# Where two gates get their sigmoid, and which of seven products waits for the last input: a hybrid attention and recurrence layer

## The chip, the cores and the metric

The kernel runs on one core of a Trainium2 chip. The metric is the time of one execution in microseconds (us); every time below is of the device. A core has engines that run at the same time and meet through semaphores: PE (TensorE, matrix products; PEld is its weight load), ACT (ScalarE, activation functions and copies), DVE (VectorE, elementwise), POOL (GpSimd, elementwise and some DMAs) and SP, which only issues DMAs. Each engine works through its own queue strictly in order. ACT computes a function from a table that has to be loaded first; a load shows in the profile as ACT_TABLE_LOAD.

## The reference, cut to what matters

One layer over 1024 tokens of width 1024. One input projection feeds everything; the parts that the change touches are the two SiLU gates `silu(g) = g * sigmoid(g)` and the last projection.

```python
h = rms_norm(h_res, norm_w[layer])
z = einsum('bsd,dc->bsc', h, w_in)                       # one projection, cut into pieces
qkv_a, g_a, q_b, zf_fwd, zf_bwd, i_b, g_b, zgate_a, zgate_b = split(z, split_points)
# (A) three groups of dilated window attention, q and k RMS-normed, merged by their denominators
y_a = einsum('bsc,cd->bsd', o_a * silu(g_a), w_proj_a)
# (B) gated linear recurrence with heads of 128, forward and backward, in chunks
f = lb + (1.0 - lb) * sigmoid(z_f); log_f = log(f)       # its decay, used through exp
o_b = rms_norm(o_fwd + o_bwd, hg_norm_w) * silu(g_b)
y_b = einsum('bsc,cd->bsd', o_b, w_proj_b)
merged = sigmoid(zgate_a) * y_a + sigmoid(zgate_b) * y_b
h_res = h_res + einsum('bsd,de->bse', merged, w_out)
```

## The kernel before

**Precision and pages.** Every wide product is made in three: both operands are split into a high part (a copy by ACT into a reduced format: `whi`, `xh`) and a low part (the difference, by POOL, DVE or ACT with a DMA: `wlo`, `xl`), and PE multiplies high by high, high by low and low by high. Weights come in pages of 128 by 512; nine split pages stand ready (`RING`).

**The order is planned at build time.** The class `Plan` (L115) keeps a model clock for each engine, and `Builder` emits instructions by it: work that hangs on other engines is a task with a priority, given out by `tick` (L263) when the model says that its inputs are about ready. Small products of PE are put between the large ones by `burst` (L279) under the same rule, with a slack of 0.6 us. On the chip the emitted order is fixed; only semaphores delay it. The model gives a change of ACT's table 1.28 us (`note`, L141), and counts `exp` as served by the set that also has `ln`.

**Stages**, by the time in the profile:

1. 0 to 150 us: normalisation of the input, values of attention.
2. The block stage, 149.6 to 730.2 us (`run_quads`, L444). 24 blocks of the projection, each made by Strassen's scheme in Winograd's form: seven products instead of eight (`11`, `T1`, `T2`, `21`, `T3`, `22`, `T4`), in PSUM banks named qA, qE and qC. Three products share one bank, so `T2` may only start when ACT has copied `11` out of it. Weight sums on DVE (`qraw`) go ahead of the split. Twelve blocks are queries and keys (`put_qk`): each quarter of the block goes through a square, a head sum on PE (`nss`), an inverse root by `Ln` and `Exp` on ACT (`guess`, L1090; both write `ny`) and a Newton step on DVE (L1097). Six blocks are merge gates, stored raw (`put_sg`, L1116). Four blocks are the SiLU gate of the recurrence (`gb`) and two that of attention (`ga`), the last two of the stage: for these `put_ga` (L1129) sends each of the 24 quarters through a sigmoid on ACT and a product on DVE (`ga_sig`, L1143), and then to DRAM (`gaD`, `gbD`).
3. Attention, 747 to 945 us, with large products of the next stage's inputs between its small ones (`gp` groups on PE).
4. The merge of the three groups, up to 1034 us (`merge_load`, L1474): eight pieces, each with three loads and the gate from `gaD`, into `oaD`.
5. The recurrence, 1040 to about 1355 us. Eight heads, each about 36 us. On ACT a head is: four sigmoids over `sk` and, after a preload of the set that has `ln` and `exp`, four `Ln` (both in `logs`, L1676), sixteen `Exp` for keys and queries (`exps_b`, L1705: `km`, `qr`, `q`), and in the output norm twice a `Ln` and an `Exp` of 128 by 4 (`oy`). PE turns keys (`kT`), makes states (`U`), cross terms (`X`, `Y`) and outputs (`oB`), and `out_transpose` (L1913) takes the output (`onT`) times the gate loaded into one of two `gb` buffers (L1612). Other rings: eight `qr`, four `km`. Between them PE runs `gp` groups of 24 products.
6. 1355 to 1583 us: the rest of the merge gates, the attention projection, then the projection of the recurrence and the output projection, each by seven products in the order `SEVEN` (L1999; `seven_weights`, `seven_sides` and `seven`, L2018 to L2097). The first writes `sA` and `sE`; its quarters times their gates, added to the other branch's, are the tiles `ma`, inputs of the second. `seven_sides(M)`, which splits these, is called after all of the first projection has been emitted (L2233).

Of the kernel before, what the change touches and what calls it, by code (L numbers as in the profile page):

```python
# [583 lines left out]
def hybrid_block(ctx, tc, a, out):  # L584
# [530 lines left out]

    def put_sg(w, j):  # L1116
        def f(half, col, z, mine):
            ring = stage
            if not mine:
                ring, ps, z = blk["spare"], z, blk["spare"].get()  # L1120
                a_.activation(z, ps, AF.Copy)

            def out():
                s_.dma_start(sgD[w, j + col, half], z)
                ring.done(z)
            b.task("sp", [z], out, 1)
        return f

    def put_ga(j, dst=None):  # L1129
        dst = gaD if dst is None else dst  # L1130

        def f(half, col, z, mine):
            ring = stage
            if not mine:
                ring, ps, z = blk["spare"], z, blk["spare"].get()
                a_.activation(z, ps, AF.Copy)
            b.task("act", [z], lambda: ga_sig(dst[j + col, half], z, ring), 3, blk["y"].soon)
        return f

    def put_gb(pr):  # L1140
        return put_ga(2 * pr, gbD)

    def ga_sig(dst, z, ring):  # L1143
        t = blk["y"].get()
        a_.activation(t, z, AF.Sigmoid)

        def mul():
            v_.tensor_tensor(z, z, t, op=OP.mult)
            blk["y"].done(t)
            b.task("sp", [z], out, 1)  # L1150

        def out():
            s_.dma_start(dst, z)
            ring.done(z)
        b.task("dve", [t], mul, 3)

# [238 lines left out]
    def merge_maybe(now=False):  # L1395
        if mer or not (now or len(stored) == 48) or not att:
            return
        if now:
            b.drain()
        b.eager, b.SLACK = False, 0.6  # L1400
        psum(3)
        actx.close()
        mer["p"] = mctx.enter_context(tc.tile_pool(name="merge", bufs=1))
        mer["sel"] = sel = mer["p"].tile([16, 4, 128], F32R, name="sel")
        half = lambda k: ident[0:16, 8 * k:8 * k + 8].rearrange("p (a j) -> p a j", a=4)[:, :, :, None].to_broadcast([16, 4, 2, 64])
        v_.tensor_tensor(sel.rearrange("p a (j c) -> p a j c", j=2), half(0), half(1), op=OP.add)
        mer["og"] = b.ring(mer["p"], "og", 6, [128, 512])
        mer["gal"] = b.ring(mer["p"], "gal", 2, [128, 512])
        merge_start()

# [213 lines left out]
    IG = {}  # L1624
    GB = {}
    H = {}
# [42 lines left out]
    def start_head(h):  # L1669
# [35 lines left out]
    def exps_b(h, d, u, D1, Q2):  # L1705
# [199 lines left out]
    def scale_out(h, u, ps, on, r):  # L1905
        for c in range(4):
# [91 lines left out]

    SEVEN = ("11", "21", "T2", "T1", "T3", "22", "T4")  # L1999

    def near(tiles):
# [4 lines left out]

    def in_order(work):

# [6 lines left out]
        for k, (op, eng, ready, f) in enumerate(work):  # L2015
            b.task(eng, [], lambda f=f: go(f), 2 + 0.1 * SEVEN.index(op), lambda k=k, ready=ready: at[0] == k and ready())

    def seven_weights(base, pages, along=None):  # L2018
        raw = {}
# [4 lines left out]

        for op in SEVEN:
            for i in range(4):
# [15 lines left out]

        for op in SEVEN:
            for i in range(4):
                split(op, i)
        in_order(work)

    def seven_sides(X):
        pairs, work, mixes, did, s2, spent = {}, [], [], set(), {}, set()

        def free2(i):
            if i in spent:
                acc.done(s2[i])
# [13 lines left out]
        def mix(op, i, dst, x, y, how, after=()):  # L2067
            def f():
                if op == "T2":
                    s2[i] = acc.get()  # L2070
                if op == "T2":
                    v_.scalar_tensor_tensor(s2[i], X[*x, i], -1.0, X[*y, i], op0=OP.mult, op1=OP.subtract)
# [3 lines left out]
                if op == "22":  # L2076
# [3 lines left out]
            mixes.append((op, "dve", lambda: all((*k, i) in X for k in at) and all((m, i) in pairs for m in after)  # L2080
                          and near([X[*k, i] for k in at]) and (op != "T2" or acc.soon()), f))

        for op, a, kh in (("11", 0, 0), ("21", 0, 1), ("T2", 0, 0), ("T1", 1, 0), ("T3", 0, 0), ("22", 0, 1), ("T4", 1, 1)):
            for i in range(4):
                split(op, kh, a, i)
# [3 lines left out]
        for i in range(4):  # L2089
            mix("22", i, (0, 1), (0, 1), "s2", OP.add, ("21",))  # L2090
        for i in range(4):
            mix("T1", i, (1, 0), (1, 0), (1, 1), OP.subtract)
        in_order(work)
        in_order(mixes)
        return pairs

    def seven(base, pairs, tok, A, E, kept, fin, ready):  # L2097

# [32 lines left out]

        for o, op in enumerate(SEVEN):
            for u in range(4):
# [56 lines left out]
    b.low = "dve"  # L2190
    seven_weights(b.ops, quad[0], {"11": obs})
    pairs_b = seven_sides(X)

# [14 lines left out]
    pos += 8  # L2208
    seven_weights(b.ops + 28, quad[1])

    def fin_b(half, c, u, t, bank_):
# [24 lines left out]

    def x_load(u):
        t = sgr.get()
        s_.dma_start(t, a["x"][4 + u, :, 0:512])
        xr[u] = t  # L2240
# [4 lines left out]
    def fold(op, u, t):  # L2245
        half, e = {"11": (0, 0), "T1": (1, 1)}.get(op, (0, 1))

        def f():
            more(t, a["x"][4 * half + u, :, 512 * e:512 * e + 512])
            folded.add((op, u))  # L2250
# [5 lines left out]
    def fin_o(half, e, u, t, bank_):  # L2256
        r0 = 128 * (4 * half + u)
        ring, o = acc, t
# [10 lines left out]
        def late():  # L2269
            more(o, a["x"][u, :, 512:1024])  # L2270
            b.task("sp", [o], out_, 1)
# [4 lines left out]

    seven(b.ops + 28, pairs_o, True, b.bank, b.gps, fold, fin_o, lambda op, u: (op, u) in folded)
    b.drain()
# [103 lines left out]
```

## Time and profile before

| | us |
|---|---|
| three runs | 1585.03, 1586.14, 1587.09 (median 1586.14) |
| the profiled execution | 1584.98, of which the span from first to last instruction 1583.2 |
| PE busy in the span | 1489.0 (94%) |
| ACT busy | 994.3 (63%), in it 107 table loads: 137.3 |
| DVE busy | 975.7 (62%) |
| POOL busy | 365.6 (23%) |

Busy is the time in which an engine had at least one instruction running; a row of the groups gives an instruction's tiles (written before the arrow, read after it), its shape, its count, busy time, the mean of one in ns, and the idle time of the engine just ahead of it with what ended that. A row of the windows gives start and end, length, then the busy time and count of each engine, the mean granted PE clock (1.00 is full), the DMA share and GB/s. A wait reads "who <- what ended it: total us, times, longest".

### The profile page before, as it was taken

To read this page: it belongs to the slowest core of one execution; us is meant where nothing else is said; L and a number is where in the kernel's file an instruction comes from. 1 tells how busy PE (TensorE), PEld (TensorE's weight loads), DVE (VectorE), ACT (ScalarE), POOL (GpSimd) and SP (SyncE) were. 2 spreads that over 40 slices of the span, in tenths; PEclk is the share of its full clock that TensorE was granted. 3 is DMA by queue.
4 is the path that set the end of the run, shared out by engine and by line. 5 is a ranking of instruction groups with operands and counts; after the bars stand their busy time and mean duration, and the time that the engine had idled before them with its cause. 6 is when DMAs were issued, how large, how long until landed. Compare 5 with 4: busy or idle time off the path is not lost.

```text
span 1583.2 us, 23063 instructions
## 1 busy us (share of the span) xinstructions
PE 1489.0 (94%) x7965; PEld 1216.0 (77%) x7965; DVE 975.7 (62%) x1890; ACT 994.3 (63%) x1963; POOL 365.6 (23%) x376
## 2 busy tenths in 40 slices
PE   8999999798798889689999999999999999998998
PEld 7788887576676667567888878788888888876787
DVE  6792676466556767563554332628888877358873
ACT  5543667667767788774676762157877875546451
POOL 0032344244232322122030032332222222000011
PEclk9999999899999999899999999999999999999999
DMA  5365466455313323127654446863446443664554
GB/s 192 131 197 194 162 200 135 140 133 113 107 67 107 100 57 103 47 80 235 217 195 160 134 133 165 249 178 87 121 100 166 108 120 101 207 223 148 166 143 131
DMA packets 193578, 227.76 MB, mean 144 GB/s; under 512 B 45563, under 2 KB 118291, under 8 KB 192948
## 3 DMA queue, kind: packets, MB, share of 16 engines
q1 hardware_dynamic: 174084, 204.06, 39.6%
q0 software_dynamic: 11952, 21.76, 8.8%
q10 hardware_dynamic: 7424, 0.45, 0.3%
q8 instruction: 63, 1.03, 0.3%
q14 instruction: 55, 0.45, 0.1%
HBM read 166.08 MB, written 81.63 MB: 156 GB/s over the span
## 4 chain that ended last, share of the span: by engine, by line
PE 58%; ACT 9%; issue 4%; DVE 4%; DMA 1%; SPq 0%; POOL 0%; ACTq 0%; DVEq 0%; POOLq 0%
PE gp L57 26%; PE qA L57 7%; PE sA L57 5%; PE sE L57 3%; ACT L57 3%; PE o L57 3%; ACT ny L57 3%; PE oB L57 2%; PE qE L57 2%; PE sc L57 2%; PE pT L57 2%; ACT whi L57 1%; PE U L57 1%; PE qC L57 1%; PE X L57 1%
## 5 line engine op out<-in xcount | busy, mean ns | idle before, releaser
L57 POOL TENSOR_TENSOR wlo<-qraw,whi 128x512 fp32r<-128x512 f32 x120 | 170.5, 1427 | 403.2 <-ACT whi L57 376.8
L57 ACT ACTIVATE whi<-qraw 128x512 fp32r<-128x512 f32 x168 | 103.1, 624 | 66.0 <-DVE qraw L57 36.2
L57 ACT ACT_TABLE_LOAD x107 | 137.3, 1283 | 8.6 <-PE gp L57 5.5
L57 PE MATMUL gp<-hh,whi 128*128 128x512 f32 x336 | 138.3, 412 | 0.7 <-ACT stage L57 0.7
L57 PE MATMUL gp<-hh,wlo 128*128 128x512 f32 x336 | 131.6, 392 | 0.0
L57 PE MATMUL gp<-hl,whi 128*128 128x512 f32 x336 | 131.1, 390 | 0.0
L57 POOL TENSOR_TENSOR wlo<-raw,whi 128x512 fp32r<-128x512 f32 x48 | 65.8, 1379 | 235.0 <-ACT whi L57 232.8
L57 DVE CUSTOM_DVE_ANT_0 as<-sc,abias 128x192 f32<-128x192 f32 (+2 forms) x192 | 56.1, 348 | 100.4 <-PE sc L57 79.8
L57 DVE TENSOR_TENSOR qraw<-qraw,qraw 128x512 f32<-128x512 f32 x96 | 81.9, 854 | 44.5 <-POOL wlo L57 41.6
L57 PE MATMUL gp<-whi,hh 128*128 128x512 f32 x248 | 100.9, 407 | 2.1 <-ACT hh L57 1.5
L57 ACT ACTIVATE stage<-gp 128x512 f32<-128x512 f32 x60 | 35.4, 594 | 103.8 <-PE gp L57 60.1
L57 PE MATMUL gp<-whi,hl 128*128 128x512 f32 x248 | 97.3, 392 | 1.4 <-DVE hl L57 1.3
L57 PE MATMUL gp<-wlo,hh 128*128 128x512 f32 x248 | 96.8, 390 | 0.0
L57 ACT ACTIVATE whi<-raw 128x512 fp32r<-128x512 f32 x104 | 64.9, 626 | 47.2 <-PE gp L57 33.8
L57 ACT ACTIVATE as<-as,neg 128x192 f32<-128x192 f32 (+2 forms) x192 | 83.5, 440 | 5.6 <-DVE neg L57 5.6
L57 DVE TENSOR_TENSOR wlo<-qraw,whi 128x512 fp32r<-128x512 f32 x48 | 33.4, 696 | 79.3 <-ACT whi L57 79.2
L57 PE MATMUL qA<-hh,whi 128*128 128x512 f32 x192 | 77.3, 403 | 3.1 <-DVE spare L57 2.0
L57 DVE SCALAR_TENSOR_TENSOR ny<-ny,spare 128x512 f32<-128x512 f32 x48 | 76.1, 1585 | 1.6
L57 PE MATMUL qA<-hh,wlo 128*128 128x512 f32 x192 | 76.5, 398 | 0.0
L57 PE MATMUL qA<-hl,whi 128*128 128x512 f32 x192 | 76.5, 398 | 0.0
L57 PEld LDWEIGHTS gp<-hh,whi 128*128 128x128 f32 x336 | 63.2, 188 | 14.9 <-issue 2.0
L57 PEld LDWEIGHTS gp<-hh,wlo 128*128 128x128 f32 x336 | 63.1, 188 | 14.0
(298 smaller groups left out, 4193.0 us busy)
## 6 DMA issues: line engine op xcount, KB each, us to landing
raw<-in_w_in_dram SPq DMA_DIRECT2D x96, 256.0 KB, 3.2
qraw<-in_w_in_dram SPq DMA_DIRECT2D x96, 256.0 KB, 3.8
qkD<-ny SPq DMA_DIRECT2D x48, 256.0 KB, 2.6
sg<-sgD SPq DMA_DIRECT2D x32, 256.0 KB, 2.6
eraw<-wsD SPq DMA_DIRECT2D x32, 256.0 KB, 2.8
wlo<-in_w_in_dram POOLq DMA_DIRECT2D x31, 256.0 KB, 4.3
sgD<-stage SPq DMA_DIRECT2D x26, 256.0 KB, 2.7
ak<-qkD SPq DMA_DIRECT2D x6, 1024.0 KB
```

Of the source, the lines that this page charges most:

```text
L57: got = f(*args, **kw)
```

## The change

Four things are done.

1. **The block stage stores all gates raw.** `ga_sig` is gone; `put_ga` and `put_gb` do what `put_sg` does.
2. **The attention gate's sigmoid and product move into the merge** (`ga_load`): after the load, a sigmoid into one of two new `gas` buffers and a product in place, on ACT and DVE, eight times. They wait until the merge weights are ready.
3. **The recurrence gate's sigmoid and product move into the recurrence** (`gate`, `gates`): in `logs` of the next head, if the gate is loaded by then, between that head's sigmoids and the preload; otherwise as a task of its own, later. The sigmoid's output takes a buffer of `Bc`, which the scans use. The output product waits for `GI`. Head 7 has its gate after its exponentials.
4. **The output projection's quarters are renamed** (halves of the tokens and of the width are exchanged, `1 - half`, `1 - c`, with the weights' pages), its seven products have an order of their own, `LATER`, and its `seven_sides` is called ahead of the first projection's `seven`; the operand of `T2` goes into a tile of the first projection that is free by then.

```diff
-    for k, (w, step, at) in enumerate(((wpb, 2, lambda kh, c: 8 * c + kh), (wo, 1, lambda kh, c: 8 * c + 4 * kh))):
+    for k, (w, step, at) in enumerate(((wpb, 2, lambda kh, c: 8 * c + kh), (wo, 1, lambda kh, c: 8 * c + 4 * (1 - kh)))):
...
-            b.task("act", [z], lambda: ga_sig(dst[j + col, half], z, ring), 3, blk["y"].soon)
...
-    def ga_sig(dst, z, ring):
-        t = blk["y"].get()
-        a_.activation(t, z, AF.Sigmoid)
...
+    put_sg = lambda w, j: put_raw(lambda col, half: sgD[w, j + col, half])
+    put_ga = lambda j: put_raw(lambda col, half: gaD[j + col, half])
+    put_gb = lambda k: put_raw(lambda col, half: gbD[2 * k + col, half])
...
         def ga_load():
-            ld[3] = mer["gal"].get()
-            s_.dma_start(ld[3], gaD[p, half])
+            t = mer["gal"].get()
+            s_.dma_start(t, gaD[p, half])
+            b.task("act", [t], lambda: ga_sig(t), 3, lambda: "ab" in mer and mer["gas"].soon())
...
+    def gate(h, u):
+        t = hp.tile([128, 512], F32, tag="Bc", name=b.name("gs"), bufs=2)
+        a_.activation(t, GB[h, u], AF.Sigmoid)
+        b.task("dve", [t], lambda: (v_.tensor_tensor(GB[h, u], GB[h, u], t, op=OP.mult), GI.add((h, u))), 3)
+
+    def gates(h):
+        for u in range(2):
+            here = lambda u=u: (h, u) in GB and b.when_all([GB[h, u]])
+            if here():
+                gate(h, u)
+            else:
+                b.task("act", [], lambda u=u: gate(h, u), 4, here)
...
     def logs(h):
         for d, u in ORDER:
             a_.activation(SK[h, d, u], SK[h, d, u], AF.Sigmoid)
+        if h:
+            gates(h - 1)
         a_.preload_act_table_set("natural_log_exp_and_others")
...
+        if h == 7 and len(st["QR"]) == 4:
+            gates(h)
...
-                  lambda: stage.soon() and (h, u) in GB and b.when_all([GB[h, u]]), merge=False)
+                  lambda: stage.soon() and (h, u) in GI and b.when_all([GB[h, u]]), merge=False)
...
+    LATER = ("11", "T2", "21", "T1", "T3", "22", "T4")
...
-            M[half, c, u] = ma
+            M[1 - half, 1 - c, u] = ma
...
-    seven(b.ops, pairs_b, False, b.gps, b.bank, lambda *_: None, fin_b, None)
-    pairs_o = seven_sides(M)
+    pairs_o = seven_sides(M, LATER, lambda i: X[0, 0, i])
+    seven(b.ops, pairs_b, SEVEN, False, b.gps, b.bank, lambda *_: None, fin_b, None)
```

Over the whole program ACT's queue had 107 table loads and has 62. In the block stage 85 become none; in the recurrence (from the first sigmoid over `sk` to the last `oy`) 16 become 57; elsewhere six become five. PE's queue is as long in both.

**Block stage, ACT.** The first inverse root after the first gate sigmoid, before (`ny` from `nss` is `Ln`, `ny` from `ny` is `Exp` and then a square):

```order
L57 ACTIVATE ny_2268<-spare_2197 128x512
L57 ACTIVATE nhi_2269<-ny_2268 128x512
L57 ACTIVATE spare_2288<-qA_2272 128x512
L57 ACTIVATE whi_2290<-qraw_1961 128x512
L57 ACT_TABLE_LOAD
L57 ACTIVATE ny_2303<-nss_2294,eps 128x512
L57 ACT_TABLE_LOAD
L57 ACTIVATE ny_2303<-ny_2303 128x512
L57 ACTIVATE ny_2304<-ny_2303 128x512
```

and the same place now:

```order
L57 ACTIVATE ny_2256<-spare_2186 128x512
L57 ACTIVATE nhi_2257<-ny_2256 128x512
L57 ACTIVATE spare_2276<-qA_2260 128x512
L57 ACTIVATE whi_2278<-qraw_1961 128x512
L57 ACTIVATE ny_2291<-nss_2282,eps 128x512
L57 ACTIVATE ny_2291<-ny_2291 128x512
L57 ACTIVATE ny_2292<-ny_2291 128x512
```

The two loads at each of 40 inverse roots are gone, and so are five at the gates.

**Recurrence, ACT, after the four `Ln` of a head.** Before, the key copies and then the exponentials:

```order
L57 ACTIVATE qr_9499<-sk_9401,lbv,omlb 128x512
L57 ACTIVATE kT_9535<-kT_9530 128x512
L57 ACTIVATE sk_9543<-gp_9481 128x512
L57 ACTIVATE km_9621<-qr_9493,lomlb 128x4x64
L57 ACTIVATE km_9621<-q_4_9550,lomlb 128x4x64
```

and now, with the two gates of the head before (`gs`):

```order
L57 ACTIVATE kT_10333<-kT_10328 128x512
L57 ACTIVATE sk_10360<-gp_10311 128x512
L57 ACT_TABLE_LOAD
L57 ACTIVATE gs_10362<-gb_10247 128x512
L57 ACTIVATE whi_10408<-raw_10025 128x512
L57 ACTIVATE wlo_10409<-whi_10408 128x512
L57 ACTIVATE gs_10416<-gb_10322 128x512
L57 ACT_TABLE_LOAD
L57 ACTIVATE km_10418<-qr_10277,lomlb 128x4x64
```

The gate comes after the preload, so the table is changed to the sigmoid and back. In the output norm of the same heads `Ln` and `Exp` stood side by side before:

```order
L57 ACTIVATE on_9750<-oB_9738 128x512
L57 ACTIVATE sk_9758<-gp_9701 128x512
L57 ACTIVATE oy_9762<-ssb_9760,eps 128x4
L57 ACTIVATE oy_9762<-oy_9762 128x4
L57 ACTIVATE oz_9763<-oy_9762 128x4
```

and now have a load each:

```order
L57 ACTIVATE on_10094<-oB_10082 128x512
L57 ACT_TABLE_LOAD
L57 ACTIVATE oy_10105<-ssb_10103,eps 128x4
L57 ACT_TABLE_LOAD
L57 ACTIVATE oy_10105<-oy_10105 128x4
L57 ACTIVATE oz_10106<-oy_10105 128x4
```

Heads 2 to 7 have eight loads each for two before, and the last gate brings five more.

**The seam between the last two projections, ACT.** Before, the gates' sigmoids (`sg`) and weight splits come first, and all splits of `ma` after them:

```order
L57 ACTIVATE sg_13816<-sg_13816 128x512
L57 ACTIVATE whi_13857<-eraw_13730 128x512
L57 ACTIVATE sg_13840<-sg_13840 128x512
L57 ACTIVATE whi_13878<-eraw_13754 128x512
L57 ACTIVATE whi_13898<-eraw_13778 128x512
L57 ACTIVATE whi_13918<-eraw_13802 128x512
L57 ACTIVATE whi_13938<-eraw_13826 128x512
L57 ACTIVATE xh_13952<-ma_12818 128x512
L57 ACTIVATE xh_13956<-ma_12835 128x512
```

and now the first splits of `ma` stand among the sigmoids:

```order
L57 ACTIVATE sg_13720<-sg_13720 128x512
L57 ACTIVATE xh_13747<-ma_13106 128x512
L57 ACTIVATE xh_13754<-ma_13130 128x512
L57 ACTIVATE whi_13768<-eraw_13629 128x512
L57 ACTIVATE sg_13744<-sg_13744 128x512
L57 ACTIVATE xh_13779<-ma_13151 128x512
L57 ACTIVATE whi_13793<-eraw_13648 128x512
L57 ACTIVATE xh_13815<-ma_13171 128x512
```

The output projection's first four inputs are split some ten ACT instructions earlier.

**In the first of the two projections, ACT.** Before, the fourth input of its third product (`xh` from `acc`) stands behind gate sigmoids:

```order
L57 ACTIVATE sg_13395<-sg_13395 128x512
L57 ACTIVATE sg_13419<-sg_13419 128x512
L57 ACTIVATE sg_13430<-sg_13430 128x512
L57 ACTIVATE xh_13443<-acc_13434 128x512
L57 ACTIVATE xh_13457<-ob_13112 128x512
```

and now ahead of them:

```order
L57 ACTIVATE xh_13372<-acc_13347 128x512
L57 ACTIVATE whi_13376<-eraw_13345 128x512
L57 ACTIVATE whi_13389<-eraw_13356 128x512
L57 ACTIVATE sg_13367<-sg_13367 128x512
L57 ACTIVATE whi_13417<-eraw_13383 128x512
```

The sum on DVE that it splits has moved up with it.

More of the change, by code (lines that the diff above doesn't have):

```diff
@@ L1123, in out @@
             def out():
-                s_.dma_start(sgD[w, j + col, half], z)
+                s_.dma_start(dst(col, half), z)
                 ring.done(z)
@@ L1488, in ga_load, with ga_sig, ga_mul @@
         def ga_load():
-            ld[3] = mer["gal"].get()
-            s_.dma_start(ld[3], gaD[p, half])
+            t = mer["gal"].get()
+            s_.dma_start(t, gaD[p, half])
+            b.task("act", [t], lambda: ga_sig(t), 3, lambda: "ab" in mer and mer["gas"].soon())
+        def ga_sig(t):
+            g = mer["gas"].get()
+            a_.activation(g, t, AF.Sigmoid)
+            b.task("dve", [g], lambda: ga_mul(t, g), 3)
+        def ga_mul(t, g):
+            v_.tensor_tensor(t, t, g, op=OP.mult)
+            mer["gas"].done(g)
+            ld[3] = t
         for g in range(3):
@@ L1624, in hybrid_block @@
     IG = {}
-    GB = {}
+    GB, GI = {}, set()
     H = {}
@@ L2005, in more, with in_order @@
         g_.dma_start(dst, src, accum_op=OP.add)
-    def in_order(work):
+    def in_order(work, order):
         at = [0]
@@ L2015, in in_order, with seven_weights @@
         for k, (op, eng, ready, f) in enumerate(work):
-            b.task(eng, [], lambda f=f: go(f), 2 + 0.1 * SEVEN.index(op), lambda k=k, ready=ready: at[0] == k and ready())
-    def seven_weights(base, pages, along=None):
+            b.task(eng, [], lambda f=f: go(f), 2 + 0.1 * order.index(op), lambda k=k, ready=ready: at[0] == k and ready())
+    def seven_weights(base, pages, order, along=None):
         raw = {}
@@ L2023, in load @@
             s_.dma_start(raw[m, i], pages[m][i])
-        for op in SEVEN:
+        for op in order:
             for i in range(4):
@@ L2041, in split, with seven_sides @@
                          and b.split_next == k and k < b.freed + b.RING, f))
-        for op in SEVEN:
+        for op in order:
             for i in range(4):
                 split(op, i)
-        in_order(work)
-    def seven_sides(X):
+        in_order(work, order)
+    def seven_sides(X, order, other=None):
         pairs, work, mixes, did, s2, spent = {}, [], [], set(), {}, set()
         def free2(i):
-            if i in spent:
+            if i in spent and other is None:
                 acc.done(s2[i])
@@ L2069, in f @@
                 if op == "T2":
-                    s2[i] = acc.get()
-                if op == "T2":
+                    s2[i] = other(i) if other else acc.get()
                     v_.scalar_tensor_tensor(s2[i], X[*x, i], -1.0, X[*y, i], op0=OP.mult, op1=OP.subtract)
@@ L2080, in mix @@
             mixes.append((op, "dve", lambda: all((*k, i) in X for k in at) and all((m, i) in pairs for m in after)
-                          and near([X[*k, i] for k in at]) and (op != "T2" or acc.soon()), f))
-        for op, a, kh in (("11", 0, 0), ("21", 0, 1), ("T2", 0, 0), ("T1", 1, 0), ("T3", 0, 0), ("22", 0, 1), ("T4", 1, 1)):
+                          and near([X[*k, i] for k in at]) and (op != "T2" or (near([other(i)]) if other else acc.soon())), f))
+        at = {"11": (0, 0), "21": (0, 1), "T2": (0, 0), "T1": (1, 0), "T3": (0, 0), "22": (0, 1), "T4": (1, 1)}
+        for op in order:
             for i in range(4):
-                split(op, kh, a, i)
+                split(op, at[op][1], at[op][0], i)
         for i in range(4):
@@ L2088, in seven_sides, with seven @@
             mix("T2", i, "s2", (1, 1), (0, 0), OP.subtract)
[L2089 to L2094, printed above, removed]
+        late = [lambda i=i: mix("22", i, (0, 1), (0, 1), "s2", OP.add, ("21",)) for i in range(4)]
+        soon = [lambda i=i: mix("T1", i, (1, 0), (1, 0), (1, 1), OP.subtract) for i in range(4)]
+        for f in late + soon if order is SEVEN else soon + late:
+            f()
+        in_order(work, order)
+        in_order(mixes, order)
         return pairs
-    def seven(base, pairs, tok, A, E, kept, fin, ready):
+    def seven(base, pairs, order, tok, A, E, kept, fin, ready):
         bankA, bankE, p, q, r = {}, {}, {}, {}, {}
@@ L2130, in evac @@
                 fin(1, 0, u, bankA[u], A)
-        for o, op in enumerate(SEVEN):
+        for o, op in enumerate(order):
             for u in range(4):
@@ L2248, in f @@
         def f():
-            more(t, a["x"][4 * half + u, :, 512 * e:512 * e + 512])
+            more(t, a["x"][4 * (1 - half) + u, :, 512 * e:512 * e + 512])
             folded.add((op, u))
@@ L2256, in fin_o @@
     def fin_o(half, e, u, t, bank_):
-        r0 = 128 * (4 * half + u)
+        r0 = 128 * (4 * (1 - half) + u)
         ring, o = acc, t
@@ L2269, in late @@
         def late():
-            more(o, a["x"][u, :, 512:1024])
+            more(o, a["x"][4 + u, :, 512:1024])
             b.task("sp", [o], out_, 1)
@@ L2275, in fin_o @@
             b.task("sp", [o], out_, 1)
-    seven(b.ops + 28, pairs_o, True, b.bank, b.gps, fold, fin_o, lambda op, u: (op, u) in folded)
+    seven(b.ops + 28, pairs_o, LATER, True, b.bank, b.gps, fold, fin_o, lambda op, u: (op, u) in folded)
     b.drain()
```

29 lines of the change are left out of this document (6 added, 23 removed).

## The prediction, on record before the run

> **What bounds the kernel now.** I read the busy time by stage first. The columns are: stretch, length, then busy time and count of PE, PEld, DVE, ACT and POOL, then the mean granted PE clock, the DMA share and GB/s.
>
> ```profile
> core 0: us, PE busy (x) PEld busy (x) DVE busy (x) ACT busy (x) POOL busy (x), PEclk, DMA share, GB/s
> 149.60:250.00 100.40, 100.40 (x441) 82.53 (x440) 67.58 (x85) 64.75 (x110) 42.59 (x34) 1.00 0.63 186
> 250.00:730.20 480.20, 407.34 (x1675) 326.03 (x1674) 293.29 (x342) 353.10 (x506) 155.58 (x122) 0.94 0.38 101
> 945.00:1040.00 95.00, 94.31 (x402) 73.34 (x401) 42.31 (x58) 22.35 (x42) 31.05 (x25) 1.00 0.68 204
> 1040.00:1411.00 371.00, 369.18 (x2392) 315.74 (x2391) 258.99 (x555) 262.11 (x546) 74.69 (x124) 1.00 0.50 134
> 1411.00:1583.20 172.20, 160.60 (x673) 128.29 (x671) 120.35 (x192) 77.63 (x137) 10.36 (x12) 0.97 0.52 158
> ```
>
> PE sets the end, and loses time in one place. In the first 100 us of the block stage 441 products take 100.4 us: 0.2277 us each, with PE never idle. The next 1675 would take 381.4 us at that pace and take 480.2: **98.8 us lost**, 72.9 as idle time (480.2 - 407.3), the other 25.9 mostly at a lower clock (0.94). The recurrence loses almost nothing, the last stage some 12 us.
>
> Next, the waits of PE from 149.6 to 730.2 us:
>
> ```profile
> PE qA L57 <- ACT stage L57: 23.1, 6, 6.2
> PE nss L57 <- ACT whi L57: 18.6, 3, 9.3
> PE nss L57 <- DVE ny L57: 14.6, 5, 5.4
> PE qA L57 <- ACT spare L57: 10.1, 5, 2.5
> ```
>
> ACT is named for 51.8 of the 72.9 us. The timeline of one such wait says why:
>
> ```profile
> 512.02 1.28 ACT L57 ACT_TABLE_LOAD   x1
> 513.32 1.30 ACT L57 ACTIVATE ny<-ny 128x512 f32<-128x512 f32 x2
> ...
> 515.63 1.28 ACT L57 ACT_TABLE_LOAD   x1
> ...
> 517.63 1.28 ACT L57 ACT_TABLE_LOAD   x1
> 518.92 1.29 ACT L57 ACTIVATE ny<-ny 128x512 f32<-128x512 f32 x2
> 520.12 0.58 ACT L57 ACTIVATE stage<-qA 128x512 f32<-128x512 f32 x1
> 520.75 0.79 PE L57 MATMUL qA<-S2h,whi 128*128 128x512 f32 x1 [6.15 <-ACT stage L57]
> ```
>
> PE waits 6.15 us for a bank whose copy (0.58 us) is queued behind two inverse roots with two loads each. The groups of ACT in the whole stage have
>
> ```profile
> L57 ACT ACT_TABLE_LOAD x85 | 109.1, 1283 | 1.5
> ```
>
> and up to 247.9 us, when the second load begins,
>
> ```profile
> L57 ACT ACTIVATE ny<-nss,eps 128x512 f32<-128x512 f32 x8 | 5.4, 677 | 0.0
> L57 ACT ACT_TABLE_LOAD x2 | 2.6, 1283 | 0.0
> ```
>
> This is a control inside the trace: eight inverse roots without a load while PE ran dense; the other forty, with loads, fall in the stretch that loses. The planner charges a change from sigmoid to `Ln` once, five there and five back; 75 of the 85 loads are not in its plan: 75 x 1.283 = 96.2 us, about what is lost.
>
> **The change, part by part.** *Block stage.* ACT loses 85 loads (109.1 us) and 24 sigmoids of some 0.63 us (15): 64.8 + 353.1 - 124 = 294 us of work for 482 us of dense PE. At most the whole 98.8 us comes back. At least what ACT is named for does, with its share of the slow clock: 51.8 x 98.8 / 72.9 = 70.2 us. The waits on DVE partly come from late ACT results, so I take half of the difference: **-85 us** (70 to 99). DVE also loses 24 products of 0.95 us. Stores and loads of the gates are the same in number, so SP's queue carries nothing new; a stage buffer is free sooner, straight after its store.
>
> *Merge.* Eight sigmoids and eight products, some 5 and 8 us, on engines that the row from 945 to 1040 us shows busy 22 and 42 of 95 us while PE runs its large groups. They are hidden by these. Without the cover, one piece's chain of some 2 us stands ahead of the last merge products: **+1 us** (0 to 2).
>
> *Recurrence.* Seven heads, then a head's dense part and its loose part on ACT, then the price of a sigmoid:
>
> ```profile
> 1080.00:1334.00 254.00, 252.91 (x1808) 219.49 (x1808) 209.56 (x462) 195.50 (x422) 59.80 (x101) 1.00 0.45 117
> 1192.00:1215.60 23.60, 23.60 (x179) 20.60 (x176) 20.69 (x44) 22.02 (x51) 6.54 (x11) 1.00 0.49 126
> 1215.60:1228.00 12.40, 12.40 (x94) 10.88 (x93) 9.75 (x25) 5.42 (x10) 1.86 (x3) 1.00 0.76 191
> L57 ACT ACTIVATE sk<-sk 128x512 f32<-128x512 f32 x28 | 15.4, 619 | 0.1
> ```
>
> A head takes 36.3 us and ACT works 27.9 of it. Heads 2 to 7 get six more loads and two sigmoids: 6 x 1.283 + 2 x 0.62 = 8.9 us, so **ACT's work becomes 36.8 us for 36.3**. The room is 8.4 us a head, but in the wrong place: 1.6 us in the dense part, 7 in the part where ACT waits for PE. Queued behind each load, on ACT, are the exponentials that make `km` and so `kT`, `X` and `U`, and the evacuations of `gp`; PE waits for those. Floor: 36.8 - 36.3 for six heads, 3 us. Ceiling: all 41 loads and 16 sigmoids (62.5 us) at the block stage's rate, 98.8 lost per 124 of ACT: 50 us. For the value: of a head's six loads the plan counts three (to the sigmoid, to `Exp`, to `Ln`); the other three, and three at the last gate, are 21 x 1.283 = 27 us that its order does not know. The block stage paid for such loads nearly one to one; the loose part takes back a little: **+25 us** (3 to 50). DVE gains two products a head, on 82% busy. The new wait of `onT` for the gate's product, with the `gp` products behind it on PE, is in this price, and so is that of the sigmoid for a `Bc` buffer.
>
> Two rules of the Trainium skill give another price. "ScalarE: Activation LUTs", section "Table sets: the hidden batching unit", has `ln` then `exp` in one load, since one set holds both; by it a gate would cost about two loads, the recurrence nothing, and the sum would be 25 us lower. The rows of ACT's order contradict it: each pair has two. The same page, section "What ACT_TABLE_LOAD costs", adds a drain of about 1.38 us to each switch; by it 41 more loads would cost 57 us more. Here the load of 512.02 us ends at 513.30 and its successor starts at 513.32.
>
> *The seam.*
>
> ```profile
> 1497.58 0.40 PE L57 MATMUL sA<-xh,wlo 128*128 128x512 f32 x1
> 1498.98 0.51 PE L57 MATMUL sA<-whi,xh 128*128 128x512 f32 x1 [1.00 <-ACT xh L57]
> ...
> 1504.31 0.39 PE L57 MATMUL sA<-whi,xl 128*128 128x512 f32 x1
> 1440.38 0.63 ACT L57 ACTIVATE sg<-sg 128x512 f32<-128x512 f32 x1 [1.40 <-DMA sg<-sgD]
> 1440.91 0.61 ACT L57 ACTIVATE xh<-acc 128x512 fp32r<-128x512 f32 x1
> 1441.58 0.79 PE L57 MATMUL sA<-xh,whi 128*128 128x512 f32 x1 [5.42 <-ACT xh L57]
> ```
>
> From 1497.58 to 1504.31 twelve products take 6.73 us instead of 2.73, because the splits of `ma` start late. Now they stand early, and the quarter that comes last enters with the third product, 96 products (22 us) in: **-4 us** (0 to 4). The second place is the first projection's third product, whose fourth input waits behind a sigmoid whose own load is late. Now the sigmoids stand behind it: 5.4 us and some clock, at most 5.42 x 98.8 / 72.9 = 7.3. I take **-5 us** (0 to 7), as it rests on when the loads land.
>
> *Sum* against the profiled execution's 1584.98 us: -85 + 1 + 25 - 4 - 5 = -68, so 1517. That execution lies 1.2 us under the median of the three runs, so **1518 us**.
>
> **Rivals.** *DVE becomes the block stage's bound.* Its costly groups there:
>
> ```profile
> L57 DVE TENSOR_TENSOR qraw<-qraw,qraw 128x512 f32<-128x512 f32 x92 | 78.1, 849 | 28.5 <-POOL wlo L57 25.6 <-DMA qraw<-in_w_in_dram 2.9
> L57 DVE SCALAR_TENSOR_TENSOR ny<-ny,spare 128x512 f32<-128x512 f32 x48 | 76.1, 1585 | 1.6
> L57 DVE SCALAR_TENSOR_TENSOR spare<-spare,nqk,ny 128x512 f32<-128x512 f32 x48 | 48.6, 1013 | 0.0
> L57 DVE TENSOR_TENSOR nlo<-ny,nhi 128x512 fp32r<-128x512 f32 x48 | 41.9, 883 | 8.3 <-ACT nhi L57 8.3
> L57 DVE SCALAR_TENSOR_TENSOR ny<-nss,ny 128x512 f32<-128x512 f32 x48 | 33.0, 688 | 53.4 <-ACT ny L57 53.3
> L57 DVE TENSOR_TENSOR wlo<-qraw,whi 128x512 fp32r<-128x512 f32 x47 | 32.7, 696 | 78.5 <-ACT whi L57 78.5
> ```
>
> A query or key block needs (76.1 + 48.6 + 41.9 + 33.0) / 12 = 16.6 us for its norm, (78.1 + 32.7) / 24 = 4.6 for weights, and three sums at 0.69: 23.3 us, where PE needs 84 + 8 products, 20.9. If the gate blocks between them do not absorb it, 12 x 2.4 = 29 us stay lost; I forecast 14, so 1533. Against it: the first 100 us hold a pair of such blocks and lost nothing.
>
> *The recurrence pays its ceiling*, 50 instead of 25: 1543 us. For it: 36.8 us of work in 36.3 leaves ACT no time to wait for anyone.
>
> *Slower than before: heads no longer overlap.* `logs` needs four of eight `qr` buffers, which the outputs of an earlier head return. Now that is the head before last. The dense part that starts at 1192 us reads a previous head's second output at
>
> ```profile
> 1203.45 0.60 ACT L57 ACTIVATE on<-oB 128x512 f32<-128x512 f32 x1
> ```
>
> If late exponentials made each head wait for the outputs of the one just before it, a head would last 36.3 + 11.5 + 8.9 = 56.7 us: 20.4 more, 122 in six heads, against 25 in my sum: 1615 us. It decides from (85 + 9 - 1) / 6 = 15 us a head on; the slack in this loop is now a whole head, so it is unlikely.
>
> *The loads come back in the block stage* and nothing is gained: 1586 us. ACT's order speaks against it.
>
> **How the numbers follow.** Forecast 0.62, DVE 0.14, ceiling 0.15, no overlap 0.06, no gain 0.03. The forecast's own ends are 1480 (99, 4 and 7 gained, 3 paid) and 1566 (70 gained, 50 and 2 paid); both at once is rare, and 8 times in 10 I expect 1488 to 1550, which holds the second and third cases. Faster by over 0.2% (about what a measurement of this kernel tells from no change): 0.62 + 0.14 + 0.15 = 0.91; the same 0.03; slower 0.06.
>
> **What would show it.** The block stage ends near 644 us, without a load in it, ACT about 61% busy, and PE has no wait of over 3 us for a bank's copy; waits on `ny` or `nlo` that add up to over 25 us would mean the second case. In the recurrence 57 loads, a head of about 40 us, ACT over 90% busy, and new PE waits on `kT`, `X`, `U` or `onT` of 2 to 4 us a head; waits under 5 us in all, or over 40, would show the price wrong. At the seam no wait of PE over 0.5 us. The whole is wrong if the block stage still loses over 35 us, or the recurrence lasts over 60 us longer.

## The result and the profile after

The changed kernel takes 1510.13 us (median of four runs, 1507.86 to 1511.62), the kernel before 1586.62 (four runs, 1585.03 to 1587.30): a ratio of **0.9518 [0.9502, 0.9535]**. It is faster by 76 us; 1518 us was forecast, in a range of 1488 to 1550.

First the stages. In the windows of before, the whole block stage and the recurrence (from the first `kT` to the first `sA`) read

```profile
149.60:730.10 580.50, 507.64 (x2114) 408.50 (x2113) 360.86 (x426) 417.79 (x614) 198.17 (x156) 0.95 0.42 115
1077.60:1411.00 333.40, 331.58 (x2226) 284.64 (x2225) 245.25 (x525) 233.15 (x495) 63.58 (x104) 1.00 0.48 132
```

and in the windows of the changed kernel the block stage, attention with the merge, the recurrence and the last stage, and then five heads alone:

```profile
148.90:631.00 482.10, 481.74 (x2114) 396.42 (x2113) 342.23 (x403) 295.38 (x507) 201.11 (x156) 1.00 0.51 139
631.00:980.50 349.50, 346.08 (x2332) 278.80 (x2331) 159.68 (x576) 197.75 (x590) 70.49 (x77) 1.00 0.58 182
980.50:1346.70 366.20, 344.65 (x2226) 289.33 (x2225) 256.09 (x541) 293.90 (x552) 63.50 (x104) 0.98 0.43 121
1346.70:1509.80 163.10, 157.06 (x673) 125.59 (x671) 118.76 (x192) 77.08 (x137) 10.38 (x12) 1.00 0.54 165
1020.00:1225.00 205.00, 188.18 (x1260) 158.70 (x1259) 154.29 (x332) 182.76 (x341) 42.91 (x72) 0.97 0.40 105
```

| stage | before | after | difference | forecast |
|---|---|---|---|---|
| start | 149.6 | 148.9 | -0.7 | 0 |
| block stage | 580.5 | 482.1 | **-98.4** | -85 |
| attention and merge | 347.5 | 349.5 | +2.0 | +1 |
| recurrence | 333.4 | 366.2 | **+32.8** | +25 |
| last stage | 172.2 | 163.1 | **-9.1** | -9 |
| span | 1583.2 | 1509.8 | -73.4 | -68 |

The two profiled executions are 73 us apart and the medians 76: that of before lies 1.6 us under its median, that of after (1511.62) 1.5 over.

**The block stage** is now PE alone: the same 2114 products, 481.74 us busy of 482.1 at full clock, and ACT works 295.38 us for 417.79 (61% of the stage). Of the 98.4 us, 72.5 were idle time of PE (72.9 before, 0.4 now), and 25.9 are the same products running faster (507.64 us busy before), at a clock of 1.00 for 0.95. The only wait of PE in it, in the form "who <- what ended it: total us, times, longest", is

```profile
PE qA L57 <- ACT stage L57: 0.4, 2, 0.2
```

Among the groups of ACT in this stage there is no table load any more. On DVE, the Newton step behind each inverse root waits far less for its input:

```profile
L57 DVE SCALAR_TENSOR_TENSOR ny<-nss,ny 128x512 f32<-128x512 f32 x48 | 32.9, 686 | 7.5 <-ACT ny L57 7.5
```

7.5 us of idle time where it was 53.4: DVE had been late because ACT was.

**The recurrence** has its loads now. The groups of ACT there:

```profile
L57 ACT ACT_TABLE_LOAD x56 | 71.8, 1283 | 3.5 <-DMA gb<-gbD 2.5
L57 ACT ACTIVATE gs<-gb 128x512 f32<-128x512 f32 x16 | 9.8, 625 | 0.1
```

56 loads for 15 in these windows. From the first sigmoid to the last `oy` it is 57 for 16: each window leaves out the first two of these and holds one behind the last `oy`. The longest waits of PE there are

```profile
PE U L57 <- ACT kT L57: 6.7, 4, 3.7
PE kT L57 <- DVE sk L57: 5.9, 3, 2.7
PE oB L57 <- DVE S L57: 4.5, 5, 1.4
PE onT L57 <- ACT on L57: 2.2, 2, 1.2
PE Y L57 <- DVE xa L57: 1.0, 1, 1.0
```

PE is idle for 366.2 - 344.65 = 21.6 us where it was 1.8 (19.7 more), and the same 2226 products take 13.1 us longer at a clock of 0.98. That is the whole of the 32.8. The clock by itself makes about half of the 13.1 (an estimate: 331.58 / 0.98 is 6.8 us more than 331.58); the rest stays open. A head lasts about 205.0 / 5 = 41.0 us, and ACT is busy for 182.76 / 205.0 = 89% of it. The timeline of ACT ahead of the longest of these waits:

```profile
1086.03 1.28 ACT L57 ACT_TABLE_LOAD   x1
1087.32 0.30 ACT L57 ACTIVATE oy<-ssb,eps 128x4 f32<-128x4 f32 x1
1087.64 1.28 ACT L57 ACT_TABLE_LOAD   x1
1088.93 0.21 ACT L57 ACTIVATE oy<-oy 128x4 f32<-128x4 f32 x1
...
1090.96 1.28 ACT L57 ACT_TABLE_LOAD   x1
...
1092.57 1.28 ACT L57 ACT_TABLE_LOAD   x1
...
1095.84 0.57 ACT L57 ACTIVATE kT<-kT 128x512 f32<-128x512 f32 x1
1096.47 1.44 PE L57 MATMUL U<-ig,kT 128*128 128x128 f32 x5 [3.68 <-ACT kT L57]
```

Four loads (5.1 us) between 1086.03 and 1093.85 us stand on ACT ahead of the copy of the keys for which `U` waits. The two ahead of `oy` are the `Ln` and `Exp` that stood side by side in one set before.

**The last stage** waits no longer at the junction of the two projections, nor for 5.42 us in the first of them. The waits that are left stand in the first projection and are small:

```profile
PE sE L57 <- DVE xl L57: 1.1, 3, 0.6
PE sE L57 <- ACT xh L57: 1.1, 2, 0.5
```

### The profile page after: what moved, and what is told of

Its sections match the earlier page's. It is cut to its first block, busy times and chain, and to the rows that moved or that the text cites. A ratio compares the mean times of both kernels' runs of the same rounds, so it can differ in the third digit from the quotient of the medians.

```text
span 1509.8 us, 23030 instructions
## 1 busy us (share of the span) xinstructions
PE 1473.4 (98%) x7965; PEld 1206.7 (80%) x7965; DVE 974.0 (65%) x1890; ACT 935.3 (62%) x1918; POOL 369.3 (24%) x376
## 4 chain that ended last, share of the span: by engine, by line
PE 77%; ACT 11%; DVE 7%; issue 2%; DMA 2%; POOL 1%; SPq 0%; ACTq 0%; DVEq 0%; POOLq 0%
PE gp L57 27%; PE qA L57 15%; PE qE L57 7%; PE sA L57 6%; PE sE L57 4%; PE qC L57 4%; ACT L57 3%; PE o L57 3%; PE sc L57 2%; PE pT L57 2%; PE oB L57 2%; PE u L57 1%; PE nss L57 1%; ACT sk L57 1%; DVE ny L57 1%
## 5 line engine op out<-in xcount | busy, mean ns | idle before, releaser
L57 POOL TENSOR_TENSOR wlo<-qraw,whi 128x512 fp32r<-128x512 f32 x120 | 174.6, 1465 | 300.1 <-ACT whi L57 254.0
L57 DVE TENSOR_TENSOR qraw<-qraw,qraw 128x512 f32<-128x512 f32 x96 | 85.0, 886 | 34.9 <-POOL wlo L57 24.7
L57 PEld LDWEIGHTS gp<-hl,whi 128*128 128x128 f32 x336 | 63.9, 190 | 10.6
L57 DVE SCALAR_TENSOR_TENSOR ny<-ny,spare 128x512 f32<-128x512 f32 x48 | 70.8, 1475 | 1.6
```

Of the source, the lines that this page charges most:

```text
L57: got = f(*args, **kw)
```

## The experiments

All ratios are to the kernel before on the same chip. Not all kernels ran on one chip, so two of them are best compared by their ratios. The stages, from one profiled execution of each kernel (us, table loads in brackets):

| kernel | median | ratio [95%] | block stage | recurrence | last stage |
|---|---|---|---|---|---|
| before | 1586.62 | 1 | 580.5 (85) | 333.4 (15) | 172.2 |
| after | 1510.13 | 0.9518 [0.9502, 0.9535] | 482.1 (0) | 366.2 (56) | 163.1 |
| exp_gate | 1485.97 | 0.9372 [0.9348, 0.9397] | 482.3 (0) | 333.5 (15) | 172.2 |
| loads_back | 1631.70 | 1.0291 [1.0262, 1.0320] | 598.1 (85) | 365.1 (56) | 163.4 |
| plan_before | 1540.85 | 0.9711 [0.9694, 0.9728] | 532.9 (87) | 333.5 (15) | 173.3 |
| exp_rec | 1490.16 | 0.9407 [0.9391, 0.9423] | 482.8 (0) | 343.1 (16) | 166.1 |
| preload | 1502.92 | 0.9481 [0.9465, 0.9497] | 482.5 (0) | 351.2 (41) | 169.7 |
| gate_next | 1484.59 | 0.9363 [0.9349, 0.9377] | 482.9 (0) | 338.6 (22) | 163.3 |
| gb4sk6 | 1501.78 | 0.9472 [0.9457, 0.9487] | 482.0 (0) | 352.9 (21) | 166.0 |
| no_seam | 1515.14 | 0.9560 [0.9540, 0.9579] | 482.3 (0) | 366.2 (56) | 165.6 |
| seam_only | 1581.74 | 0.9976 [0.9966, 0.9986] | 580.5 (85) | 333.4 (15) | 170.1 |
| best | 1480.02 | 0.9350 [0.9336, 0.9364] | 482.5 (0) | 334.4 (19) | 163.4 |

### Block stage: the loads or the work?

**exp_gate** is the kernel before with another function at the same place. All its work stays, the loads go.

```diff
     def ga_sig(dst, z, ring):
         t = blk["y"].get()
-        a_.activation(t, z, AF.Sigmoid)
+        a_.activation(t, z, AF.Exp)
```

> The kernel before, with Exp in place of Sigmoid in the two gates of the block stage: the same 24 ACT passes and 24 DVE products in the same place, but no change of table (107 loads become 21). The gates' values are not the reference's. Theory A, the loads are what the block stage loses by: the stage takes 483 to 490 us for 580.6 and the whole about 1488 us. Theory B, the sigmoid and product work and the stage buffer held by it are: no difference, about 1586 us.

The window of its block stage, and the one wait of PE in it:

```profile
148.70:631.00 482.30, 481.85 (x2114) 396.41 (x2113) 361.06 (x426) 308.94 (x529) 203.09 (x155) 1.00 0.53 139
```

```profile
PE qA L57 <- ACT stage L57: 0.5, 2, 0.3
```

The 24 activations and 24 products of the gates are all there, DVE is even as busy as before (361.06 us for 360.86), and PE is as dense as in the changed kernel. The gates' work cost nothing; the loads cost all of the 98 us.

**loads_back** is the changed kernel with a sigmoid of one column after each raw gate quarter, so that the table changes as it did.

```diff
+    def put_tiny(dst):
+        def f(half, col, z, mine):
+            raw(half, col, z, mine)
+            b.task("act", [], lambda: a_.activation(tinys, half_ones[:, 0:1], AF.Sigmoid), 3)
+        raw = put_raw(dst)
+        return f
+
+    tinys = consts.tile([128, 1], F32, name="tinys")
-    put_ga = lambda j: put_raw(lambda col, half: gaD[j + col, half])
-    put_gb = lambda k: put_raw(lambda col, half: gbD[2 * k + col, half])
+    put_ga = lambda j: put_tiny(lambda col, half: gaD[j + col, half])
+    put_gb = lambda k: put_tiny(lambda col, half: gbD[2 * k + col, half])
```

> The changed kernel, with a sigmoid of 128 by 1 into a spare tile after each of the 24 raw gate quarters of the block stage: 86 loads come back there, nearly no work does. Theory A (the loads): the block stage goes back to about 575 us and the whole to about 1605 us. Theory B (the moved work): the stage stays near 485 us, the whole near 1512 us.

The window of its block stage, and the longest waits of PE there:

```profile
149.70:747.80 598.10, 525.15 (x2114) 415.99 (x2113) 339.24 (x403) 408.13 (x614) 200.08 (x155) 0.94 0.42 112
```

```profile
PE nss L57 <- DVE ny L57: 28.2, 5, 6.9
PE nss L57 <- ACT whi L57: 17.8, 4, 4.5
PE qA L57 <- ACT stage L57: 13.5, 4, 3.5
PE qA L57 <- ACT spare L57: 13.0, 6, 3.5
```

85 loads bring all of the loss back, and 17.6 us more than before had. DVE has 24 products fewer than in exp_gate (339.24 us for 361.06) and is named for 28.2 us of PE's waits, where in exp_gate it is named for none: its lateness is that of the inverse roots it waits for: ahead of the Newton step it is idle for 38.4 us for ACT's `ny`, where exp_gate has 7.5. Why the same number of loads costs 17.6 us more in this order than before was not followed further.

**plan_before** is the kernel before with a planner that knows that `Ln` and `Exp` each change the table, unless the set with both was loaded by name. The emitted order then allows for the loads; their number hardly changes.

```diff
-            self.table = "exp" if args[0].startswith("exp") else "ln"
+            self.table = "exp" if args[0].startswith("exp") else "both"
...
-                need = {AF.Sigmoid: ("sig",), AF.Ln: ("ln",), AF.Exp: ("exp", "ln")}.get(args[2])
+                need = {AF.Sigmoid: ("sig",), AF.Ln: ("ln", "both"), AF.Exp: ("exp", "both")}.get(args[2])
```

> The kernel before, with a planner that knows what ACT really loads (ln and exp are in one set only after a preload, else one load each): same work, 109 loads for 107, another order. If the block stage loses because its plan does not count 75 of the 85 loads: most of the 98 us come back, 1500 to 1530 us. If the loads cost by their place on ACT whatever the plan knows: within 15 us of before, 1570 to 1600 us.

Its block stage, and what PE waits for most there:

```profile
149.60:682.50 532.90, 496.46 (x2114) 402.68 (x2114) 361.33 (x426) 417.20 (x616) 208.49 (x156) 0.96 0.47 126
```

```profile
PE qA L57 <- ACT stage L57: 16.1, 4, 9.0
PE nss L57 <- DVE nlo L57: 11.3, 5, 4.4
```

This is a result between the two clean answers. With 87 loads and the same work the stage loses 532.9 - 482.1 = 50.8 us where it lost 98.4. So in this one order about half of the loss goes back to the first order's ignorance of the loads, which two lines of the planner would have mended, and the other half stays with the loads. Per load: 98.4 / 85 = 1.16 us unknown to the plan, 50.8 / 87 = 0.58 known to it. The halves are rough: loads_back shows that the same number of loads can differ by 17.6 us from one order to another.

### Recurrence: the loads, the moved work, or the gate's place?

**exp_rec** is the changed kernel with another function in `gate`: the activations, the products and the waits for them stay, the loads go.

```diff
     def gate(h, u):
         t = hp.tile([128, 512], F32, tag="Bc", name=b.name("gs"), bufs=2)
-        a_.activation(t, GB[h, u], AF.Sigmoid)
+        a_.activation(t, GB[h, u], AF.Exp)
```

> The changed kernel with Exp in place of Sigmoid in the recurrence's gate: the same passes, products, buffers and waits, without the 41 loads (22 in all for 62). The gate's values are not the reference's. Theory A, the loads are the recurrence's 33 us: the recurrence takes 334 to 340 us and the whole about 1480 us. Theory B (the moved work, the Bc buffers, the wait of onT for its gate): 366 us and 1510 us.

Its recurrence, and the largest wait of PE there:

```profile
980.00:1323.10 343.10, 335.37 (x2225) 284.16 (x2224) 255.27 (x541) 243.74 (x512) 62.57 (x104) 1.00 0.51 129
```

```profile
PE Y L57 <- DVE xa L57: 5.8, 6, 1.0
```

Of the 32.8 us, 366.2 - 343.1 = 23.1 go with the 40 loads (0.58 us each); 9.7 stay with the moved work in this order, 5.8 of them a wait of up to 1.0 us for DVE, six times. So neither theory had it right: the stage lies above the 334 to 340 us of the first and far under the 366 of the second.

**preload** loads the set with both functions right after a gate that runs as a task of its own, so that the `Ln` and `Exp` behind it share it.

```diff
             else:
-                b.task("act", [], lambda u=u: gate(h, u), 4, here)
+                b.task("act", [], lambda u=u: (gate(h, u), a_.preload_act_table_set("natural_log_exp_and_others")), 4, here)
```

> The changed kernel, with a preload of the set of ln and exp behind each gate sigmoid that is given out on its own: 45 loads for 62, and all of them in the plan. Theory A, the recurrence's 33 us come from the loads, 41 more than before at 0.8 us each: 24 more than before cost 19 us, the whole about 1496 us; if only loads that the plan does not count cost, almost nothing is left, about 1480 us. Theory B, the moved sigmoids, products and buffers cost: no difference, about 1510 us.

Its recurrence, and PE's waits there:

```profile
979.90:1331.10 351.20, 337.56 (x2225) 285.87 (x2224) 256.78 (x541) 275.09 (x537) 63.01 (x104) 0.99 0.47 125
```

```profile
PE gp L57 <- ACT xh L57: 5.6, 1, 5.6
PE oB L57 <- DVE S L57: 3.6, 3, 2.2
```

41 loads for 56, and 15 us less (47 in the whole program, two more than expected); the 17.8 us over the kernel before are near the 19 expected for the recurrence. A single wait of a `gp` group for `xh` is new. Part of the gain is given back behind the recurrence, where the last stage takes 169.7 us for 163.1, with this wait of PE:

```profile
PE sA L57 <- ACT xh L57: 5.7, 1, 5.7
```

It is the wait of the first projection that the changed kernel had lost. So the total gains only 6 us by the ratios and 7 by the medians.

**gate_next** gives the gate one head more time: `logs` takes the gates of the head before last, whose loads have landed by then, so that the sigmoid stands among those of `logs` and needs no change of its own. The gates of heads 6 and 7 still come behind the last exponentials, with a change of table.

```diff
-        if h:
-            gates(h - 1)
+        if h > 1:
+            gates(h - 2)
...
-            gates(h)
+            gates(6)
+            gates(7)
```

> The changed kernel, with a head's gate given out one head later, among the sigmoids of the second head after it, where its table is loaded anyway: 28 loads for 62, the same sigmoids, products and buffers; outputs wait longer for their gate. Theory A: 7 more loads than before in the recurrence cost 6 us, the whole about 1483 us. Theory B (work and buffers): about 1510 us. A third way: the later gate holds the outputs and stalls PE at onT, over 1495 us.

The window of its recurrence:

```profile
980.50:1319.00 338.50, 333.30 (x2225) 284.90 (x2224) 255.82 (x541) 248.89 (x518) 63.20 (x104) 0.99 0.49 130
```

22 loads, and the recurrence costs 5 us more than before instead of 33. The sixteen sigmoids and products are all still there. So most of the time was the price of the sigmoid's place, between two uses of the other set.

**gb4sk6** was to reach the same end by loading the gates earlier, with four buffers instead of two. The space is taken from `sk`, seven buffers to six, and from a pad of 288 bytes (`tinyPad`).

```diff
-    gb_ring = b.ring(hp, "gb", 2, [128, 512])
-    sk_ring = b.ring(hp, "sk", 7, [128, 512])
+    gb_ring = b.ring(hp, "gb", 4, [128, 512])
+    sk_ring = b.ring(hp, "sk", 6, [128, 512])
```

> The changed kernel with four gate buffers for two (and six sk buffers for seven and no pad of 288 bytes, for the space): the gate is there when the next head's sigmoids run and goes among them: 27 loads for 62. Theory A: about 1482 us. Theory B: about 1510 us. If six sk buffers are too few, PE waits at gp for them: 1490 to 1500 us.

The recurrence and PE's waits there:

```profile
980.10:1333.00 352.90, 344.67 (x2249) 290.00 (x2250) 256.81 (x545) 250.50 (x521) 64.81 (x105) 1.00 0.47 124
```

```profile
PE kT L57 <- DVE sk L57: 6.3, 7, 1.3
PE kT L57 <- POOL mm L57: 4.4, 1, 4.4
```

The added loads are nearly gone (21 for 15) and yet 19.5 us stay lost, with new waits: of `kT` for `sk`, seven times, and one long one for POOL. About 5 us of the 19.5 are no loss: 24 products of a `gp` group (2249 for about 2225) have come in from the merge, which has 24 fewer (2308 for 2332). The whole program is still 17 us slower than gate_next. Fewer loads were not enough here; the waits for `sk` point at the buffer that the keys gave up. Four gate buffers with seven of `sk` were not measured, so that is not shown.

### The seam

**no_seam** is the changed kernel without the fourth part: names, pages and order of the quarters as before, `seven_sides` after the first projection.

```diff
-            M[1 - half, 1 - c, u] = ma
+            M[half, c, u] = ma
...
-    pairs_o = seven_sides(M, LATER, lambda i: X[0, 0, i])
-    seven(b.ops, pairs_b, SEVEN, False, b.gps, b.bank, lambda *_: None, fin_b, None)
+    seven(b.ops, pairs_b, False, b.gps, b.bank, lambda *_: None, fin_b, None)
+    pairs_o = seven_sides(M)
```

> The changed kernel without its fourth part. About 1514 us if only the junction's 4 us belong to that part and the 5 us at the first projection's third product to the shifted plan, about 1519 us if all 9 us belong to it, 1510 us if none do.

**seam_only** is the kernel before with that part alone, the same lines the other way round.

> The kernel before with the fourth part of the change alone (order LATER, renamed quarters, sides planned ahead). If the last stage's 9 us come from it: about 1577 us, and no PE wait at the seam or in the third product of the first projection. If they come from the shifted plan of the earlier stages: 4 us or less, about 1583 us.

PE's waits in the last stage, of no_seam:

```profile
PE sA L57 <- ACT xh L57: 1.0, 1, 1.0
PE sA L57 <- DVE xl L57: 0.8, 1, 0.8
```

and of seam_only:

```profile
PE sA L57 <- ACT xh L57: 5.8, 1, 5.8
PE sE L57 <- ACT whi L57: 0.6, 1, 0.6
```

The two halves of the gain come apart. In no_seam the long wait of the first projection's third product is gone (it was 5.42 us) and the waits of 1.0 and 0.8 us at the junction are there: 165.6 us. In seam_only it is the other way round: 170.1. So 172.2 - 165.6 = 6.6 us come from the order as the first three parts shift it, and 2.1 (172.2 - 170.1) to 2.5 (165.6 - 163.1) from the fourth part. Whole runs put the fourth part somewhat higher: the interval of seam_only, 0.9966 to 0.9986, is 2.2 to 5.4 us, and the median of no_seam lies 5 us over that of the changed kernel (7 by the ratios). The 6.6 us are not a sure gain of those parts: preload, which differs from the changed kernel by one statement in the recurrence, has the long wait again.

### A version that beats both

**best** is gate_next, and loads the set with both functions once more behind the last gates.

```diff
             gates(6)
             gates(7)
+            b.task("act", [], lambda: a_.preload_act_table_set("natural_log_exp_and_others"), 4,
+                   lambda: all((k, u) in GI for k in (6, 7) for u in range(2)))
```

> The kernel of gate_next with one preload behind the last gates: 25 loads. If the recurrence's remaining 5 us over before are the last head's loads in its output norm: 3 fewer loads at 1.28 give about 1481 us. If they are the moved sigmoids and products: no change, about 1484 us.

The window of its recurrence:

```profile
980.30:1314.60 334.30, 331.36 (x2225) 283.92 (x2224) 255.32 (x541) 244.77 (x515) 63.18 (x104) 1.00 0.50 132
```

1480.02 us and 0.9350 [0.9336, 0.9364] of the kernel before: 27 us less than the changed kernel by the ratios, 30 by the medians. Over gate_next (0.9363 [0.9349, 0.9377]) the intervals overlap, so that step is seen in the windows alone. The recurrence is back within 1 us of its time before, with 19 loads for 15, sixteen sigmoids and sixteen products more, and PE busy for 331.36 us of 334.3.

## Why the prediction was right, point by point

**What bounds the stage: right, and shown.** exp_gate takes the loads away and nothing else, loads_back puts them back and nearly nothing else. The signs came as named, the end earlier: the stage ends at 631.0 us (644 forecast), has no load, ACT is busy 61% of it, and no wait exceeds 0.2 us.

**The term of -85 us was mis-sized by 13: it came to -98.4, 0.6 inside its upper end.** The step that failed is "so I take half of the difference". It left 14 us to waits that name DVE, but those were late ACT results throughout: the Newton step's idle time fell from 53.4 to 7.5 us, and exp_gate has the same DVE work without a wait. So "what ACT is named for" left out waits that ACT had caused; a wait that names an engine whose own input was late belongs to the one before it.

**That the block stage "paid for such loads nearly one to one" was right in size and half right in cause.** plan_before has loads that its order allows for, and still loses 51 of 98 us. The match of 96.2 us with 98.8 was in part luck: a plan that knew of the loads won back only about half.

**The merge:** +2.0 for +1, at the upper end. It was not taken apart.

**The recurrence:** +32.8 for +25, inside 3 to 50. A head became 41.0 us (about 40 forecast), ACT 89% busy (just under the 90 named), with the loads as counted. The waits on `U`, `kT` and `onT` came, 6.7 + 5.9 + 2.2 = 14.8 us or 1.9 a head, where 2 to 4 were named; `X` did not wait, and the waits of `oB` and `Y`, 5.5 us, were not named. The 40 loads came to 23.1 us, near the 25. That is luck in part, as the 25 was made of 21 uncounted loads at nearly their full 1.283 us, and no run tells counted loads from uncounted ones here. The term without a price of its own was the moved work: 9.7 us go with the sigmoids and products in an order that had no good place for them. In gate_next and best the same work costs 5 and 1 us, loads included.

**The seam:** -9.1 for -9, but split otherwise: -2.5 for the fourth part (-4 forecast) and -6.6 for the first projection's third product (-5), each inside its own bounds of 0 to 4 and 0 to 7. The 4 us held 1.86 us of idle time (1.00 and 0.85) and, for the rest, products at a lower clock (0.91 from 1490 to 1510 us). In no_seam the same two waits, 1.0 and 0.8 us, stand at a clock of 1.00, and cost less. That the first projection lost its wait was partly luck, as preload shows.

**The rivals.** DVE as the block stage's bound (23.3 us of work where PE has 20.9) fell: DVE is busy 342.23 / 482.1 = 71% of the stage and PE dense, so the gate blocks between do absorb it. Heads that no longer overlap would have shown 56.7 us a head; it is 41.0. Loads coming back in the block stage: none did.

**A slip without effect:** the forecast's own ends, added up from 1586.14 us, are 1479 and 1568, not 1480 and 1566.

**The two rules of the Trainium skill** that the prediction weighed give way to the measurement. By "ScalarE: Activation LUTs", section "Table sets: the hidden batching unit", `Ln` and `Exp` share a load and the recurrence would have cost nothing; the timeline shows a load ahead of each, and the recurrence cost 32.8 us. They do share one where the set was loaded by name: with one more such load at each late gate, preload has 15 loads fewer. The same page's section "What ACT_TABLE_LOAD costs" has a drain of about 1.38 us for each; here a load that starts at 1086.03 us and lasts 1.28 is followed by the next instruction at 1087.32.

## What to carry to other kernels

Where an in-order engine stands ahead of the one that sets the end, price what holds its queue by the stage that waits, not by its share of busy time: 85 loads on an engine that was 72% busy (417.79 of 580.5 us) cost 98 us, and the work beside them nothing. When such work has to move, move it to a place where its table is loaded anyway and its input has landed: one head later made 33 us into 5. And let the planner count what the chip really does: an order that knew of the loads lost about half as much.

## What was not expected of the hardware

A table load of 1.283 us cost the program 1.16 us in one order and 0.58 in another with about as many loads and the same work, and in loads_back 116.0 / 85 = 1.36, more than it lasts. So its price is that of the order around it. And a sigmoid over a single column, 24 times, was enough to bring the whole loss back and 17.6 us more: what the activation computes hardly mattered here, that the set changed did.
